# Two more places for weight tiles while the experts run

## The chip, the cores and the metric

One core of one Trainium2 chip runs the program. Its engines work side by side: TensorE (PE in the profile, PEld for its weight loads), VectorE (DVE), ScalarE (ACT), GpSimd (POOL), and SyncE (SP), which here issues the loads to 16 DMA engines. The metric is device time of one launch in microseconds; smaller is better.

## The reference

Two blocks of a network in float32, on 256 tokens of 1024 features and a context of 256 tokens. The first block has two layers: attention with forgetting, then a mixture of experts; retention, then a second mixture of experts. The second block has two layers that mix the tokens (a recurrence over matrices, a spatial gating unit, a convolution), each with a feed-forward; the context goes through a layer and a half of the same.

The experts are what the change is about. A router picks one of 4 groups for a token and 2 of the group's 8 experts; each of the 32 experts is a gated feed-forward of its own:

```python
pg, gi = lax.top_k(p_group, 1)
pv, pi = lax.top_k(jax.nn.softmax(e_in, axis=-1), TOP_K)
gates = pg * pv / jnp.sum(pv, axis=-1, keepdims=True)
# of each expert e, for the tokens xb that chose it:
a, b = jnp.split(xb @ w_gu[e], 2, axis=-1)      # w_gu[e] [1024, 1024]
y = (jax.nn.silu(a) * b) @ w_down[e]            # w_down[e] [512, 1024]
```

The weights of a layer's experts are 32 x 6 MiB, 192 MiB, and they are all read whatever the router picks.

## The kernel before

**Stages.** `run` traces the stages one after the other: `fox` (attention), `moe(0)`, `retention`, `moe(1)`, then the second block for the tokens. `weave` lets side work go along: while `moe(0)` runs, the context's mixing half (`mixer` in mode "f"), and while `moe(1)` runs, the context's feed-forward and the start of its second layer. The text calls this the context's work.

**Experts.** `moe` goes over the experts in 8 groups of 4 (q). For each group it gathers the chosen tokens, 32 places for each expert, features on partitions (`gather`, L895); multiplies them with `w_gu` over 8 row blocks k (L956); takes the gated hidden units (`ha`, L965 and L966), transposes them (L969, L970) and multiplies with `w_down` over 4 row blocks (L976). `combine` (L979) copies the result to SBUF as `ys`, the scaled outputs in the change's words, and adds it to the tokens' rows with a matmul (L986) and an addition (L988). For all but the last group `combine` comes in the middle of the next group's `w_gu` products. `ha` and `ys` each have a tag of their own in the pool `m2`, with two places, 2 KiB per partition each. The last group first asks whether an expert has more than 32 tokens (`overflow`, L1018), with a count that is loaded into registers at L1024; the branch is not taken on these inputs.

**Weight tiles.** Every weight is loaded by SP into a tile of [128, 2048] float32, 1 MiB. The tiles come from `wt` (L126): the pool `wp` has six places, and a load has to wait until a place is free, that is until the last matmul that reads the tile there is done. A pair of loads (`wload2`, L149, the DMA at L153) brings row block k of four experts. Three further places, those of tiles no longer needed, serve once at the start of each `moe` (`self.extra`). The context's loads (`wload`, L132, the DMA at L137) take places from the same pool, and its matmuls are those of L430, L464, L1390 and L1416. The order of loads on SP's queue is fixed when the program is built, and a load that waits holds up all loads behind it.

Of the kernel before, what the change touches and what calls it, by code (L numbers as in the profile page):

```python
# [19 lines left out]
NEG = -1e30  # L20
RS = -8192.0                    # what rsqrt's scaled form carries
NE, CAP, FF = 32, 32, 512
R0, R1, R2, R3, R4 = 1.8, 0.8, 1.0, 0.88, 0.7           # steps of other work per step of the main path
AHEAD = 200                     # instructions that what the others wait for goes ahead of
TAPS = 6                        # convolution taps between other work
PIECE, WS = 512, 6              # elements per partition split at a time; pieces on chip
# [3 lines left out]
# columns of the constant array  # L30
C_ID, C_LE, C_LT, C_GE, C_ONE = 0, 128, 256, 384, 512
C_Z, C_LOW, C_UP = 640, 768, 896          # 0 where col <= row / col >= row, else NEG
C_IOTA, C_GRP, C_I8 = 1024, 1056, 1088
C_SEL, C_OFF = 1096, 1112                 # row 32 j + i, column i; rows of scales: what to add, 1 / RS
C_COS, C_SIN, C_RET = 1116, 1372, 1628         # rotary, decay
NCST = C_RET + 4 * 384

# modulation vectors: which third of the columns of w_mod, and which two of its quarters
# [4 lines left out]
def constants():  # L43
    """Tables that depend on shapes alone."""
# [35 lines left out]
class Tags:  # L80
    """A pool, some of whose tags lie in another one under other names."""
# [10 lines left out]
class Net:  # L92
    def __init__(self, tc, I, out, es):
        self.tc, self.nc, self.I, self.out, self.es = tc, tc.nc, I, out, es
        pool = lambda n, b, **k: es.enter_context(tc.tile_pool(name=n, bufs=b, **k))
        self.cp = pool("cp", 1)
        self.wp = pool("wp", 6)
        self.sm = pool("sm", 2)
        self.dp = pool("dp", 1, space=bass.MemoryType.DRAM)
        self.pg = pool("pg", 4, space=PSUM)  # L100
        self.pm = pool("pm", 2, space=PSUM)
        self.flip, self.extra = 0, []
        self.later, self.pending, self.taken = [], [], False
        self.early, self.hold = -99, None                  # pieces of weights whose low parts GpSimd makes

# [7 lines left out]
    def bank(self):  # L113
        """One bank, from the other pool while g's are taken."""
        return self.m()[:, 0:512] if self.taken else self.g()

    def two(self, mode, apart=False):
        """Two banks."""
# [7 lines left out]
    def wt(self, name):  # L126
        """A weight tile; some lie in the places of tiles that are no longer needed."""
        if self.extra:
            return self.pre.tile([P, 2048], F32, tag=self.extra.pop(0), name=name)
        return self.wp.tile([P, 2048], F32, tag="w", name=name)  # L130

    def wload(self, src):  # L132
        """One tile of weights: rows (k p) of src on the partitions."""
# [6 lines left out]
    def wtile(self):  # L140
        """A weight tile as [P, 2, D]."""
        return self.wt("w").rearrange("p (b d) -> p b d", b=2)

    def gain(self, src, g):
        """src [D] on all partitions."""
# [3 lines left out]
    def wload2(self, src):  # L149
        """The same rows of two experts: src [2, P, 1024]."""  # L150
# [16 lines left out]
    def affine(self, o, i, scale, bias=None, eng=None):  # L167
        """o = i * scale + bias, per partition."""
# [10 lines left out]
    def split(self, pool, tag, src, shape=None, low=None):  # L179
        """src = H + L exactly, both in the tensor engine's one-pass format."""  # L180
# [12 lines left out]
    def wparts(self, w, mode):  # L193
        """Parts of a weight tile [P, k, c]: each a function of (row block, first column, last column)."""
# [15 lines left out]
    def pairs(self, a, b):  # L210
        """Products that make up a.b for operands in parts."""
        return [(a[0], b[0])] if len(a) == 1 else [(a[0], b[0]), (a[1], b[0]), (a[0], b[1])]

    def rstd(self, ss, n, eps=EPS):
        """1/sqrt(ss/n + eps)"""
# [4 lines left out]
    def rsqrt(self, h, scaled=False):  # L220
        """1/sqrt(h): a first guess from the exponent's bits, then Newton's steps. Scaled: RS times it, for one column."""
# [9 lines left out]
        for _ in range(3):  # L231
            if scaled:                  # y = c / sqrt(h) to (y h y - 3 c c) y = -2 c^3 / sqrt(h)
# [13 lines left out]
    def rms(self, x, b, junk, act=False):  # L246
        """rstd of token block b of x [P, 2, D]"""
# [12 lines left out]
    def transposed(self, xn, b, cb):  # L260
        """cb(k, psum [P, n, 128]) for the feature chunks k .. k + n of token block b of xn [P, 2, D]"""
# [7 lines left out]
    def normed(self, pool, x, g, sh, mode, junk, tag="x", first=None, xn=None):  # L269
        """Parts of (rms-normalised x, times g plus sh)^T, each [P, 8, T]; sh and g / RS [P, D].  # L270
        With first = (f, f f, f g), x is replaced by its rms norm with gain f before. Junk: [P, D], or [P, 2, D] with first."""
# [5 lines left out]
        for b in range(2):  # L277
            if b and self.pending:
                self.settle(mark)
            with self.tc.high_priority(offset=(2 - b) * AHEAD):  # L280
# [15 lines left out]
                if first is not None:  # L296
                    # x / sqrt(a); then its own rstd: 1 / sqrt(ss' / (n a) + eps) / sqrt(a)
# [21 lines left out]
    def raw(self, pool, x, g, tag="x", late=False):  # L319
        """Parts of (x times g)^T, each [P, 8, T], g [P, 8]; and the tokens' rstd, [P, 2] and along the free axis, which is  # L320
        left to the products."""
# [40 lines left out]
    def replace(self, after):  # L362
        """The replacing of x that normed has left."""
# [5 lines left out]
    def residual(self, x, o, g, b, wait):  # L369
        """x + o g, once the first tokens are through when waiting"""  # L370
# [15 lines left out]
    def sixteen(self, pool, xin, wsrc, bias, mode, rs=None):  # L386
        """16 columns wsrc [1024, 16], times the tokens' rs, plus bias [P, 16]: [P, 2, 16], in two steps."""
# [4 lines left out]
        # four groups of columns of the array side by side, each with a quarter of the products  # L392
# [24 lines left out]
    def fs(self, xin, wsrc, cb, mode, between=None, middle=None):  # L417
        """Features on partitions: cb(chunk, psum [P, T]) for each 128 columns of wsrc [1024, n]."""
# [18 lines left out]
    def ts(self, xin, wsrc, cb, mode, nk=8, width=512, fresh=False, between=None):  # L437
        """Tokens on partitions: cb(token block, first column, psum [P, width]).
        Fresh: one block of tokens before the other, which may be late."""
# [32 lines left out]
    def logsig(self, z, shape, tag):  # L472
        """log(sigmoid(z)) = min(z, 0) - log1p(exp(-|z|))"""
# [7 lines left out]
        v.scalar_tensor_tensor(c, u, -1.0, e, op0=ALU.add, op1=ALU.subtract)   # (u - 1) - e  # L481
# [29 lines left out]
    def setup2(self):  # L511
        """Small vectors that come later."""
# [16 lines left out]
        # silu(c), silu(c_ctx) as columns 2 n and 2 n + 1 of 32, for each third n of w_mod  # L529
# [36 lines left out]
    def row_vectors(self, l, pool):  # L566
        """Vectors that lie along the free axis, on all partitions."""
# [14 lines left out]
    def fox(self):  # L582
        nc, I = self.nc, self.I
        w_in, w_out = I["fox_w_in"][0], I["fox_w_out"][0]
        with ExitStack() as es:
# [9 lines left out]
            # halves of the heads  # L595
# [17 lines left out]
            # forget logits -> c = cumsum(log sigmoid)  # L613
# [21 lines left out]
            # two more rows for q and k: (c_q, 1) and (1, -c_k)  # L635
# [36 lines left out]
    def fox_heads(self, fp, f2, qa, ka, va, ot, masks):  # L672
        nc, v = self.nc, self.nc.vector
        parts = ((0, 128), (128, 384))          # query blocks with the keys they see
# [54 lines left out]
    def choose(self, mp, L):  # L729
        """L [P, 2, 40]: 4 group logits, 4 of -LOW, 32 expert logits. Membership M [P, 2, 32] of each token's two experts,  # L730
        and what the gates need: sorted logits and indices."""
# [27 lines left out]
    def spread(self, out, gi, w8):  # L759
        """[P, 2, 32] with w8 in the chosen group and 0 elsewhere."""  # L760
# [5 lines left out]
    def gates_of(self, mp, gv, gi, ev, ei):  # L766
        """p_group * p_expert / (sum of the two p_expert), at the experts' places."""
# [27 lines left out]
    def route(self, l):  # L795
        """Loads for the router of layer l."""
# [14 lines left out]
    def route_half(self, l, half, junk):  # L811
        """The router's products for one half of the features; junk [P, 512]."""
# [22 lines left out]
    def logits(self, mp):  # L835
        """The router's logits [P, 2, 40] and the tokens' rstd: products of x itself, scaled by it."""
# [11 lines left out]
    def moe(self, l):  # L848
        nc, I, x, v = self.nc, self.I, self.x, self.nc.vector
        w_gu, w_down = I["expert_w_gu"][l], I["expert_w_down"][l]  # L850
        with ExitStack() as es:
            pool = lambda n, b: es.enter_context(self.tc.tile_pool(name=n + str(l), bufs=b))
            mp, m2 = pool("mp", 1), pool("m2", 2)
            pair = lambda q, k: [self.wload2(w_gu[4 * q + 2 * j:4 * q + 2 * j + 2, k * P:(k + 1) * P, :]) for j in range(2)]
# [6 lines left out]
            # normalised tokens, without the gain  # L861
# [4 lines left out]
            # place of each token among its expert's  # L866
# [18 lines left out]
            def gather(q, n=4):  # L885
                """Tokens of 4 experts, features on partitions; after each step n chunks more."""
# [26 lines left out]
            def placed(q):  # L913
                """Gates at the tokens' places, places on partitions."""
# [13 lines left out]
            for q in range(8):  # L928
# [50 lines left out]
                def combine(y, c0, eng, sgt=sgt):  # L979
                    """Adds y, columns c0 and on, to the places' tokens."""  # L980
                    n = y.shape[1]
                    ys = m2.tile([P, n], F32, tag="ys", name="ys")
# [19 lines left out]
                # the last: one quarter of the columns after the other  # L1002
                ya, yb = y, self.m()
                for c in range(4):
# [10 lines left out]
                    if c % 2:  # L1015
                        yield

    def overflow(self, l, mp, m2, xn, gov, cnti, gain):  # L1018
        """Tokens beyond the CAP places of an expert: that expert densely over all tokens."""
# [44 lines left out]
    def retention(self):  # L1064
        nc, I, x, v = self.nc, self.I, self.x, self.nc.vector
        w_in, w_out = I["ret_w_in"][0], I["ret_w_out"][0]
        with ExitStack() as es:
# [16 lines left out]
            for dst, c0 in ((qr, 0), (kr, 1024)):  # L1084
                hold = []

                def rot(j, ps):
# [3 lines left out]
                    # halves of a head: t1 | t2  # L1091
# [10 lines left out]
            # decayed scores, keys on partitions: [k0: q0 q1 | k1: q1]  # L1102
# [14 lines left out]
            def normal(i):  # L1117
                """The parts of two heads' outputs, features on partitions."""
# [51 lines left out]
    def bn(self, src):  # L1170
        """Mean and variance along the free axis."""
# [6 lines left out]
    def centred(self, src, o):  # L1178
        """o[:, b, :] = src[b] without its mean and over its deviation along the free axis"""
# [12 lines left out]
    def mods(self, l, thirds=(0, 1, 2)):  # L1192
        """silu(c) @ w_mod + b_mod for both conditions i, in blocks of 512 columns: quarter j of third n in row
# [644 lines left out]
```

## Time and profile before

| what | value |
|---|---|
| runs | 2346.77, 2349.72, 2353.5 us; median 2349.72 |
| profiled execution | 2346.0 us from the first to the last instruction (its span); the page gives no other time of it |
| TensorE busy | 2127.2 us, 91% |
| VectorE, ScalarE, GpSimd busy | 1060.9, 695.6, 172.9 us |
| moved by DMA | 686.64 MB, mean 293 GB/s |
| issues of expert weights | 256 of `w_gu` and 112 of `w_down` of 1024 KB, 32 of `w_down` of 512 KB |

Where the experts run is seen from the first and the last matmul of L956: 214.3 to 1611.8 us, in two stages with retention between. A window row gives the length of a stretch, then the busy time and the count of instructions for PE, PEld, DVE, ACT and POOL, the granted TensorE clock as a share, the mean busy share of the 16 DMA engines (packets overlap a little, so it can come out above 1) and the rate. A wait row gives who waited, on which line, for whom, the sum in us, how many times, and the longest.

### The profile page before, as it was taken

What the parts mean: (1) busy time and instruction counts of PE and PEld (TensorE: products, weight loads), DVE (VectorE), ACT (ScalarE), POOL (GpSimd) and SP (SyncE); (2) the same over time, 40 slices, a digit from 0 to 9 for tenths busy, and PEclk for the clock granted to TensorE, in tenths of its full rate; (3) what the DMA queues carried; (4) which work ended last, traced back from release to release, by engine and by line L of the source; (5) the groups of instructions that cost most, each with busy time, mean ns of one, the idle gap of its engine ahead of it and who ended that gap; (6) DMA issues with size and microseconds to landing.
All of it is one profiled execution on the core that took longest, in us unless ns stands there. A gap on an engine that the chain in (4) does not pass through costs nothing. (4 is left out here: it accounts for less than half of the span.)

```text
span 2346.0 us, 32803 instructions
## 1 busy us (share of the span) xinstructions
PE 2127.2 (91%) x12844; PEld 1433.4 (61%) x12845; DVE 1060.9 (45%) x2513; ACT 695.6 (30%) x1420; POOL 172.9 (7%) x194
## 2 busy tenths in 40 slices
PE   8998899889877999989899999987998998998998
PEld 7765445344222776855444444334787997787997
DVE  6556053322101766531121221415778556777555
ACT  4353111211000434520000000012555554554554
POOL 1001000000000111010000000001212002102000
PEclk9999999999988999989999999999999999999999
DMA  8864999999999977579999999999756554555551
GB/s 257 313 245 166 350 399 392 369 399 378 379 409 384 323 281 246 203 268 382 391 398 393 399 390 390 367 356 346 256 162 202 188 190 156 187 181 171 192 185 63
DMA packets 305320, 686.64 MB, mean 293 GB/s; under 512 B 22056, under 2 KB 163784, under 8 KB 298888
## 3 DMA queue, kind: packets, MB, share of 16 engines
q1 hardware_dynamic: 305096, 684.45, 79.9%
q8 instruction: 103, 1.69, 0.3%
q14 instruction: 57, 0.47, 0.1%
q10 hardware_dynamic: 64, 0.03, 0.0%
HBM read 681.78 MB, written 2.62 MB: 292 GB/s over the span
## 5 line engine op out<-in xcount | busy, mean ns | idle before, releaser
L190 DVE TENSOR_TENSOR wl<-w,wh 128x512 fp32r<-128x512 f32 x574 | 396.3, 707 | 252.4 <-ACT wh L185 233.7
L185 ACT CAST wh<-w 128x512 fp32r<-128x512 f32 x600 | 364.3, 621 | 355.5 <-PE psm L430 111.6
L956 PE MATMUL psm<-w,xg 128*32 128x512 f32 x2048 | 319.8, 632 | 61.8 <-DMA w<-in_expert_w_gu_dram 55.0
L430 PE MATMUL psg<-xt,w 128*128 128x256 f32 x1056 | 235.8, 381 | 20.5 <-DMA w<-in_w_gu_dram 11.3
L430 PEld LDWEIGHTS psg<-xt,w 128*128 128x128 f32 x1056 | 198.0, 190 | 71.1 <-issue 38.6
L956 PEld LDWEIGHTS psm<-w,xg 128*32 128x32 f32 x2048 | 66.4, 112 | 270.6 <-issue 150.4
L430 PE MATMUL psg<-xh,wh 128*128 128x256 f32 x608 | 177.2, 291 | 3.9 <-ACT wh L185 2.4
L430 PE MATMUL psm<-xh,wh 128*128 128x256 f32 x640 | 179.9, 281 | 0.6 <-ACT ffh L1450 0.6
L430 PE MATMUL psm<-xh,wl 128*128 128x256 f32 x640 | 179.8, 281 | 0.0
L430 PE MATMUL psm<-xl,wh 128*128 128x256 f32 x640 | 179.7, 281 | 0.0
L430 PE MATMUL psg<-xh,wl 128*128 128x256 f32 x608 | 175.1, 288 | 2.4 <-DVE wl L190 2.4
L430 PE MATMUL psg<-xl,wh 128*128 128x256 f32 x608 | 173.8, 286 | 0.0
L976 PE MATMUL psm<-w,hT 128*32 128x512 f32 (+1 forms) x1152 | 156.7, 564 | 16.0 <-DMA w<-in_expert_w_down_dram 12.5
L430 PEld LDWEIGHTS psg<-xh,wh 128*128 128x128 f32 x608 | 118.1, 194 | 18.6 <-ACT wh L185 9.5
L430 PEld LDWEIGHTS psm<-xh,wh 128*128 128x128 f32 x640 | 120.7, 189 | 1.9 <-ACT ffh L1450 1.1
L430 PEld LDWEIGHTS psm<-xh,wl 128*128 128x128 f32 x640 | 120.6, 188 | 0.7
L430 PEld LDWEIGHTS psg<-xh,wl 128*128 128x128 f32 x608 | 118.0, 194 | 4.9 <-DVE wl L190 4.2
L430 PEld LDWEIGHTS psm<-xl,wh 128*128 128x128 f32 x640 | 120.8, 189 | 0.0
L430 PEld LDWEIGHTS psg<-xl,wh 128*128 128x128 f32 x608 | 117.9, 194 | 0.3 <-issue 0.2
L965 ACT ACTIVATE ha<-psm 128x512 f32<-128x512 f32 x16 | 9.6, 597 | 334.3 <-PE psm L956 334.3
L988 DVE TENSOR_TENSOR x<-x,psg 128x512 f32<-128x512 f32 (+1 forms) x72 | 45.1, 628 | 123.2 <-PE psg L986 123.0
L976 PEld LDWEIGHTS psm<-w,hT 128*32 128x32 f32 x1152 | 38.6, 111 | 93.2 <-issue 52.2
(497 smaller groups left out, 3263.9 us busy)
## 6 DMA issues: line engine op xcount, KB each, us to landing
w<-in_expert_w_gu_dram SPq DMA_DIRECT2D x256, 1024.0 KB
w<-in_expert_w_down_dram SPq DMA_DIRECT2D x112, 1024.0 KB
w<-in_w_gu_dram SPq DMA_DIRECT2D x66, 1024.0 KB
w<-in_w_mod_dram SPq DMA_DIRECT2D x48, 1024.0 KB
w<-in_w_in_dram SPq DMA_DIRECT2D x40, 1024.0 KB
w<-in_w_down_dram SPq DMA_DIRECT2D x33, 1024.0 KB
w<-in_ret_w_in_dram SPq DMA_DIRECT2D x24, 1024.0 KB
w<-in_fox_w_in_dram SPq DMA_DIRECT2D x16, 1024.0 KB
```

The costliest lines, as they stand in the source:

```text
L185: nc.scalar.copy(h, src)
L190: eng.tensor_tensor(l, src, h.bitcast(F32), op=ALU.subtract)
L430: self.nc.tensor.matmul(o, a, x, start=i == 0, stop=i == len(mm) - 1)
L956: nc.tensor.matmul(gu[32 * j:32 * j + 32, half * 512:(half + 1) * 512], xg[:, k, 32 * j:32 * j + 32], ws[j // 2][:, j % 2, half * 512:(hal ...
L965: nc.scalar.activation(ha, gu[:, 0:512], AF.Silu)
L976: nc.tensor.matmul(o[32 * j:32 * j + 32, :], hT[:, k, 32 * j:32 * j + 32], w(j), start=k == 0, stop=k == 3)
L988: v.tensor_tensor(o, o, ps, op=ALU.add)
```

## The change

`wt` takes its place from a list, `self.ring`, in turns. Outside of `moe` the list holds `wp` six times. In `moe` a new pool `more` with two places of a weight tile (16 KiB per partition) is opened after `mp` and `m2`, and the list is six times `wp`, then twice `more`; it is set back at the end of `moe`. `ys` takes the tag of `ha`, so its two places of 2 KiB fall away. The rest of the diff removes comments.

```diff
@@ class Net, __init__
         self.flip, self.extra = 0, []
+        self.ring, self.turn = [self.wp] * 6, 0
@@ wt
         if self.extra:
             return self.pre.tile([P, 2048], F32, tag=self.extra.pop(0), name=name)
-        return self.wp.tile([P, 2048], F32, tag="w", name=name)
+        self.turn = (self.turn + 1) % len(self.ring)
+        return self.ring[self.turn].tile([P, 2048], F32, tag="w", name=name)
@@ moe
             mp, m2 = pool("mp", 1), pool("m2", 2)
+            self.ring = [self.wp] * 6 + [pool("more", 2)] * 2
...
                     n = y.shape[1]
-                    ys = m2.tile([P, n], F32, tag="ys", name="ys")
+                    ys = m2.tile([P, n], F32, tag="ha", name="ys")
...
+            self.ring = [self.wp] * 6
```

## Rows read from the trace of the kernel before

**Rows 1.** The page: DMA share in tenths and rate, in 40 slices.
```profile
DMA  8864999999999977579999999999756554555551
GB/s 257 313 245 166 350 399 392 369 399 378 379 409 384 323 281 246 203 268 382 391 398 393 399 390 390 367 356 346 256 162 202 188 190 156 187 181 171 192 185 63
```

**Rows 2.** Windows of the first experts' stage: full stretches and dips.
```profile
205.00:220.00 15.00, 10.39 (x70) 6.78 (x74) 10.19 (x59) 5.77 (x14) 1.47 (x4) 0.70 0.24 77
235.00:255.00 20.00, 20.00 (x88) 7.86 (x86) 1.81 (x3) 2.02 (x3) 0.76 (x2) 1.00 0.75 269
255.00:425.00 170.00, 153.92 (x954) 86.54 (x954) 62.88 (x199) 31.09 (x73) 3.64 (x8) 0.99 1.02 396
425.00:445.00 20.00, 18.08 (x112) 7.05 (x104) 12.73 (x42) 6.25 (x24) 1.19 (x1) 1.00 0.76 289
575.00:580.00 5.00, 5.00 (x34) 1.59 (x35) 1.86 (x3) 0.00 (x0) 0.00 (x0) 1.00 0.62 203
605.00:610.00 5.00, 5.00 (x33) 1.51 (x35) 1.46 (x3) 0.00 (x0) 0.00 (x0) 1.00 0.45 144
610.00:770.00 160.00, 118.58 (x663) 36.66 (x656) 15.97 (x31) 9.81 (x23) 0.16 (x2) 0.88 1.03 396
```

**Rows 3.** Windows of the second experts' stage.
```profile
1009.00:1018.00 9.00, 9.00 (x63) 3.56 (x62) 4.09 (x22) 0.51 (x2) 1.47 (x4) 0.79 0.17 38
1030.00:1050.00 20.00, 20.00 (x114) 14.37 (x116) 2.06 (x6) 2.90 (x5) 0.76 (x2) 1.00 0.80 281
1075.00:1080.00 5.00, 5.00 (x41) 2.19 (x39) 0.75 (x2) 0.00 (x0) 0.00 (x0) 1.00 0.63 219
1080.00:1482.00 402.00, 372.06 (x1946) 194.63 (x1942) 86.83 (x146) 22.61 (x54) 3.03 (x8) 1.00 1.03 394
1500.00:1545.00 45.00, 41.22 (x178) 17.24 (x178) 19.60 (x37) 6.36 (x15) 4.47 (x4) 0.96 0.80 304
```

**Rows 4.** Waits of SP's queue over the whole run.
```profile
SPq L153 <- PE psm L956: 289.9, 147, 9.4
SPq L153 <- PE psg L430: 223.6, 32, 8.9
...
SPq L1024 <- DVE cnti L912: 19.5, 2, 10.3
```

**Rows 5.** TensorE's waits in 255:425, 445:575, 580:605, 610:770, 1080:1482, 1482:1632, one row each.
```profile
PE psm L956 <- DMA w<-in_expert_w_gu_dram: 5.8, 7, 1.5
...
PE psm L956 <- DMA w<-in_expert_w_gu_dram: 9.5, 9, 2.0
...
PE psm L956 <- DMA w<-in_expert_w_gu_dram: 2.6, 1, 2.6
...
PE psm L956 <- DMA w<-in_expert_w_gu_dram: 25.4, 23, 2.0
...
PE psm L956 <- DMA w<-in_expert_w_gu_dram: 11.8, 15, 1.6
...
PE psg L430 <- DMA w<-in_w_in_dram: 1.2, 1, 1.2
```

**Rows 6.** Timeline, start and length: scaled outputs read, next hidden units written.
```profile
430.20 1.98 PE L986 MATMUL psg<-ys,sgt 128*128 128x512 f32 x4
...
466.55 0.60 ACT L965 ACTIVATE ha<-psm 128x512 f32<-128x512 f32 x1 [28.72 <-PE psm L956]
```

**Rows 7.** SP's queue: the count load (min/median/max ns, first and last start), loads around it.
```profile
L1024 SPq TENSOR_LOAD <-cnti x2: 453/462/472, 215.3 to 1011.0; - x2
...
203.72 0.53 SPq L137 DMA_DIRECT2D w<-in_w_in_dram  x1
...
218.82 5.33 SPq L153 DMA_DIRECT2D w<-in_expert_w_gu_dram  x4
```

**Rows 8.** Loads of line 137 in 200:759 and in 996:1597.
```profile
L137 SPq DMA_DIRECT2D w<-in_w_in_dram x12: 367/368/1102, 203.7 to 532.1; - x12
...
L137 SPq DMA_DIRECT2D w<-in_w_gu_dram x22: 367/368/532, 999.2 to 1455.8; - x22
```

## The prediction

> **What bounds the kernel now.** I read the 40 slices first. A slice is 58.65 us. The DMA row stands at 9 in ten slices from 234 us and again in ten from 1056 us, with rates of 323 to 409 GB/s; all other slices have 313 or less [rows 1]. These two stretches are the experts' stages, with what is prefetched behind them. So if loads bound the kernel anywhere, they do it there. The windows of the first stage [rows 2] then show two kinds of stretch. In 255 to 425 the DMA share is 1.02 at 396 GB/s while TensorE is busy 153.9 of 170 us: loads set the pace. In 235 to 255, 425 to 445, 575 to 580 and 605 to 610 the share is 0.75, 0.76, 0.62 and 0.45 with TensorE busy nearly all the time: the tiles are full, TensorE is on the context's work, and nobody fetches. The second stage has the same pattern at 1009 to 1018, 1030 to 1050, 1075 to 1080 and 1500 to 1545, with 402 us at share 1.03 between [rows 3]. The waits of the DMA queue name the cause: SP stands most often at line 153, the experts' loads, until a matmul that reads an older tile is done, for L956 289.9 us and for L430 223.6 [rows 4]. TensorE's waits are the other half. After each dip it waits for weights again: 5.8 us in 255 to 425, 9.5 in 445 to 575, 2.6 in 580 to 605 and 25.4 in 610 to 770; in the second stage 11.8 in 1080 to 1482 [rows 5]. So the DMA engines idle when the six places are full, and TensorE starves a little later. What the engines fail to fetch in a dip is paid in the next starved stretch, if that is long enough.
>
> **What two more places can bring.** No load, matmul or byte is added or removed. One tile is 1 MiB, 1.0486 MB; at 396 GB/s [rows 2] it takes 2.65 us, two take 5.3. With two more places the queue runs on for up to 5.3 us into each dip. A dip gives back the smaller of 5.3 us and what it lost, once between two starved stretches. I count as lost (1.02 less the share) times the length.
> - Start of stage one, 205 to 255: 15 x 0.78 = 11.7 and 20 x 0.27 = 5.4, in all 17.1; capped at **5.3**. Spent in 255 to 425, where the waits of one line alone are 5.8 [rows 5].
> - 425 to 445: 20 x 0.26 = **5.2**, just under the cap. Spent in 445 to 575 (9.5).
> - 575 to 580: 5 x 0.40 = **2.0**. Spent in 580 to 605 (2.6).
> - 605 to 610: 5 x 0.57 = **2.9**. Spent in 610 to 770 (25.4), and from there the share is 1.03 to the stage's end [rows 2], so all that was won reaches that end.
> - Start of stage two: 9 x 0.85 = 7.7, 20 x 0.22 = 4.4 and 5 x 0.39 = 2.0, in all 14.1 with no starved stretch between; capped at **5.3**. Spent in 1080 to 1482 (11.8 on one line).
> - 1500 to 1545: 45 x 0.22 = 9.9 lost, counted as **0**. After 1482 TensorE waits for loads only 1.2 us, once [rows 5]; other work sets the pace there, and nothing is left to spend the lead on. Its bounds are 0 and the cap, 5.3; I take 0, the end that the 1.2 is nearest to.
>
> Sum: 5.3 + 5.2 + 2.0 + 2.9 + 5.3 = 20.7 us. The profiled execution spans 2346.0 us; the median of the three runs, 2349.7, is 3.7 above that, which I keep as what lies around the span. 2346.0 - 20.7 + 3.7 = **2329 us**.
>
> **What the change costs.** The scaled outputs move into the tag of the gated hidden units, so three tiles per group of four experts share two places of one size. The new neighbour costs nothing as long as each tile is read long before its place comes round again: one block of matmuls on scaled outputs starts at 430.20 and lasts 1.98 us, and the next hidden units are written at 466.55, 34 us later [rows 6]. Were that cover gone, a write would stand behind at most one such block, 2 us, sixteen times: 32 us at most, and it cannot be a gain. I take 0, the end that the 34 us speak for. The two new places lie where the part before the experts kept its last tiles, and a load into them has to wait for the readers of those. In stage one that can cost the first of the two idle stretches, 11.7, but the second, 5.4, is enough for the cap; so 0, with 5.3 as the other end if both were missed. After the stage the loads take turns on the six again. The last eight expert tiles now hold eight places instead of six, so a place among the six comes free no later than today: 0, and one tile's 2.65 us either way.
> The added wait is SP's: a load whose turn falls on the pair waits for that pair, where before any of six places did. Behind it stand all other loads, since the weights are issued on that one queue, and behind those TensorE. This is the price of the last rival.
> The first extra loads must also get past the count load (L1024), at which SP stood 19.5 us in two waits, the longer 10.3 [rows 4], until 215.3 and 1011.0; in stage one four expert loads come right after it, the first at 218.82 [rows 7]. If the extra two stay behind it, the stages' first idle stretches stay, but those of 235 to 255 and of 1030 to 1080 lie after it (5.4 and 4.4 + 2.0 us), and each still fills the cap.
> What is late next in the starved stretches is again the load, at 2.65 us each, since the lead is spent there; past 1482 us it is the context's work.
>
> **A rule that speaks against it.** The share of 1.02 to 1.03 over 160 and 402 us says that the 16 DMA engines themselves are the limit there [rows 2, 3]. The Trainium skill, Perfetto Trace Analysis, section What "DMA-bound" means, says that a kernel bound on DMA engines is helped by large descriptors; places for tiles are not in its list. By that rule alone nothing is won, and it is the second rival below. The trace agrees with it inside the full stretches, and disagrees in the dips, where the share is 0.45 to 0.76.
>
> **The rivals.**
> 1. Only the dips inside stage one pay, and the leads at the two starts are lost: TensorE is busy 20.00 of 20 us there [rows 2, 3], and if the stages are paced by TensorE for longer than the shares say, a load that is early there is early for nobody. Then 5.2 + 2.0 + 2.9 = 10.1 us: 2346.0 - 10.1 + 3.7 = 2339.6. For it: TensorE is busy 372.1 of 402 us in stage two. Against it: it still waits 11.8 us there for one kind of load.
> 2. The change doesn't do what it says: both stages take their bytes over their rate, the lead is never built or is spent on loads that nobody waits for, and the time stays at 2349.7. For it: share 1.02 to 1.03 for most of both stages. Against it: the SP waits [rows 4] and the dips.
> 3. Slower: fixed turns block the queue. The context's loads share the turns: of the two commonest kinds the queue issued 12 in stage one and 22 in stage two [rows 8]; a quarter of these 34, eight or nine, would fall on the pair. If such a tile is held long (the one issued at 203.72 [rows 7] waits for the context's first matmuls), the next turn finds one place of two, and SP stands with free places elsewhere. SP's longest single wait on a context matmul at line 153 is 8.9 us [rows 4]; less the lead of 5.3, 3.6 us each, 8.5 x 3.6 = 31 us lost against 20.7 won: 2349.7 + 10 = 2360. It decides from 20.7 / 8.5 = 2.4 us per such tile. Against it: tiles are read almost in the order of their loads, so what a turn waits for is mostly what is freed next.
>
> **How the numbers follow.** Chances: the forecast 0.60, rival 1 0.20, rival 2 0.11, rival 3 0.09. The forecast's own range is 2324 (the dip at 1500 pays its cap) to 2336 (one start's lead is lost, and 1.5 us of the others). The range reaches from 2321 to 2348, which takes in rival 1 and stops short of no change; it leaves out about 0.05 below and 0.15 above. A measurement of this kernel can tell 0.3%, 7 us, from no change, that is below 2342.7. The forecast and four fifths of rival 1 are faster: 0.76. The rest of rival 1 (its dips half filled) and rival 2 are the same: 0.15. Rival 3 is slower: 0.09.
>
> **What would show it.** In the changed profile the dip after 425 should be at a share near 1.0, those after 575 and 605 gone, and TensorE's waits on the experts' loads shorter by what the dips gave; SP's waits at line 153 should not grow in length. The first stage should end 15 us earlier and the second 21 us. The prediction is wrong if the dips are filled and the stage ends where it did (rival 2), if only the ends of the starts fail (rival 1), or if new dips appear behind a context tile in the pair (rival 3).

## The result and the profile after

The changed kernel takes 2315.39 us (median of 4 runs, 2315.31 to 2318.41). The kernel before, run beside it, takes 2348.24. The ratio is 0.9861 with the 95% interval [0.9848, 0.9874]. The forecast was 2329.0 with a range of 2321 to 2348: the direction was right, the size was not, and the time lies 5.6 us below the range. The profiled execution spans 2316.6 us against 2346.0; its own run took 2318.41.

Lines 430, 956, 976, 1024 and 153 of before are 432, 959, 979, 1028 and 155 here. First the page's DMA rows, for [rows 1]:

```profile
DMA  8875999999999877689999999998756554555551
GB/s 263 312 250 183 358 399 406 379 400 399 409 406 381 316 269 251 233 289 387 399 402 400 402 396 402 370 380 297 245 170 190 195 187 147 203 181 172 183 182 64
```

The fifth to the twelfth slice, all within stage one, had a mean of 384 GB/s and have one of 394; the mean over the run went from 293 to 296. The bytes are the same, 686.64 MB.

Windows of the changed kernel at the places of [rows 2] (same columns), shifted by what the kernel had won by then (the first two stand unshifted):

```profile
205.00:220.00 15.00, 10.82 (x66) 6.99 (x70) 9.73 (x56) 5.23 (x14) 1.47 (x4) 0.66 0.29 98
235.00:255.00 20.00, 20.00 (x87) 8.04 (x86) 1.81 (x3) 2.11 (x4) 0.96 (x3) 1.00 0.81 287
255.00:420.00 165.00, 150.77 (x958) 86.14 (x957) 63.46 (x199) 31.89 (x76) 3.46 (x7) 1.00 1.03 401
419.00:439.00 20.00, 18.42 (x108) 7.51 (x104) 12.60 (x42) 6.13 (x24) 1.18 (x1) 0.91 0.84 320
564.00:569.00 5.00, 5.00 (x31) 1.69 (x33) 2.22 (x4) 0.00 (x0) 0.00 (x0) 1.00 1.03 410
590.00:595.00 5.00, 5.00 (x31) 1.74 (x33) 2.10 (x4) 0.00 (x0) 0.00 (x0) 1.00 1.03 409
594.00:753.00 159.00, 109.54 (x678) 35.06 (x671) 16.15 (x32) 11.02 (x23) 0.16 (x2) 0.98 1.04 398
```

The dips that stood at 575 and 605 are gone (0.62 and 0.45 have become 1.03). The one at 425 is only shallower, 0.84 for 0.76. And the stretch that looked full moved as well: 401 for 396 GB/s, over 165 us in place of 170 for nearly the same work (958 and 954 matmuls).

The second stage, for [rows 3]:

```profile
992.00:1001.00 9.00, 9.00 (x73) 4.26 (x72) 4.41 (x22) 0.73 (x2) 1.47 (x4) 0.92 0.25 77
1013.00:1033.00 20.00, 20.00 (x120) 14.52 (x120) 1.45 (x4) 2.22 (x4) 0.76 (x2) 1.00 0.77 286
1061.00:1454.00 393.00, 370.47 (x1946) 194.80 (x1942) 86.74 (x146) 22.58 (x54) 3.03 (x8) 1.00 1.03 400
1472.00:1517.00 45.00, 41.35 (x183) 18.25 (x182) 19.73 (x38) 6.78 (x15) 4.47 (x4) 0.96 0.90 339
```

The third row holds the same 1946 matmuls as 1080 to 1482 of before. It takes 393 us in place of 402, at 400 GB/s in place of 394, and the share is 1.03 in both.

SP's waits (columns as in [rows 4]) and TensorE's waits on expert weights in 255:419, 439:564, 592:753 and 1061:1454 (as in [rows 5]; in 565:590 there is none):

```profile
...
SPq L155 <- PE psm L959: 214.6, 122, 9.5
SPq L155 <- PE psg L432: 157.7, 32, 10.0
...
SPq L1028 <- DVE cnti L915: 17.9, 2, 9.4
```
```profile
PE psm L959 <- DMA w<-in_expert_w_gu_dram: 5.5, 6, 1.5
...
PE psm L959 <- DMA w<-in_expert_w_gu_dram: 9.4, 8, 2.1
...
PE psm L959 <- DMA w<-in_expert_w_gu_dram: 29.0, 27, 1.5
...
PE psm L959 <- DMA w<-in_expert_w_gu_dram: 6.6, 9, 1.5
```

SP stands 75.3 and 65.9 us less at the experts' line on the two releasers shown. (The longest row of this view, line 139 on VectorE's `wl`, 515.8 us here and 506.6 before, is left out as in [rows 4]: between 200 and 760 and between 1000 and 1600 only 4.6 us of it fall, in one wait.) TensorE's waits shrink where the stage is paced by both (11.8 to 6.6). At the end of stage one they grow, 25.4 to 29.0, while the granted clock there is 0.98 in place of 0.88 and TensorE is busy 109.54 in place of 118.58 us: loads set the pace, and a faster TensorE waits longer.

**Where the time came from.** Ends of work in the two traces: the last combine of stage one 770.4 to 753.8 (16.6 us), the first matmul of stage two's experts 1010.2 to 993.5 (16.7), the last combine of stage two 1631.8 to 1602.6 (29.2), the end 29.4. So stage one gave 16.6 and stage two 12.5. Finer than that is the lead, worked out from the packets: by how much earlier the same number of bytes had landed than in the kernel before, at the times t of before. In stage one it is 6.0 us at t = 300, 8.0 at 425, 9.5 at 500, 10.2 at 575, 13.0 at 605 and 17.0 at 700. For stage two, less what the kernel had when the stage began:

| t of before, us | 1100 | 1240 | 1300 | 1400 | 1482 |
|---|---|---|---|---|---|
| changed kernel (began 16.7 early) | 6.8 | 8.7 | 9.5 | 11.3 | 12.8 |
| pair in stage two alone (1.2 late) | 6.9 | 8.9 | 9.6 | 11.4 | 13.0 |
| pair at its start alone (2.7 early) | 6.2 | 7.9 | 8.0 | 7.1 | 6.7 |
| pair from its third group on (1.5 early) | 5.7 | 5.9 | 6.6 | 8.4 | 10.0 |
| six places, new tag (1.1 early) | 0.3 | -0.5 | -1.1 | -1.5 | -1.6 |

Between its steps the lead stands still to 0.1 us over stretches of up to 60 us. So it isn't a higher rate of the DMA engines. It is a number of short holes that were there before and are not there now, inside the stretch that stood at 1.03: from 1100 to 1482 the lead grows in seven steps. At six of them the kernel before has fewer than 16 packets open (one for each DMA engine), for 0.1 to 1.8 us at a time and some 10 us in all; the changed kernel never has at the same bytes. One step, 0.4 us at 1200, shows no such hole. Two spots of the kernel before, as windows of 4 and 8 us:

```profile
1386.00:1390.00 4.00, 4.00 (x32) 1.82 (x34) 0.75 (x2) 0.00 (x0) 0.00 (x0) 1.00 0.89 336
1426.00:1434.00 8.00, 8.00 (x48) 3.66 (x47) 1.17 (x3) 0.00 (x0) 0.00 (x0) 1.00 0.86 326
```

And the same work in the changed kernel:

```profile
1360.00:1364.00 4.00, 4.00 (x35) 1.77 (x37) 0.75 (x2) 0.00 (x0) 0.00 (x0) 1.00 1.02 410
...
1398.00:1406.00 8.00, 8.00 (x49) 3.63 (x48) 1.03 (x3) 0.00 (x0) 0.00 (x0) 1.00 1.02 408
```

What makes such a hole is seen in SP's queue. Its timeline in the kernel before (start, length, what is issued):

```profile
1374.69 4.00 SPq L153 DMA_DIRECT2D w<-in_expert_w_down_dram  x3
1379.14 0.37 SPq L137 DMA_DIRECT2D w<-in_w_down_dram  x1
1387.58 3.94 SPq L153 DMA_DIRECT2D w<-in_expert_w_gu_dram  x4
1391.61 0.45 SPq L137 DMA_DIRECT2D w<-in_w_gu_dram  x1
1398.21 5.54 SPq L153 DMA_DIRECT2D w<-in_expert_w_gu_dram  x4
```

Loads go out in bunches of three to five. Between 1379.5 and 1387.6 none goes out, for 8.1 us. At 2.65 us a load that is three loads' worth. By the packets the list ran dry at 1387.9, 8.4 us after the last issue, and was full again at 1389.8, 2.2 us after the next one: with six places it held little more than three loads, and some 10 us were to be covered. The changed kernel at that spot, in the windows 1349:1361 and 1361:1364 of the view:

```profile
1349.04 0.42 SPq L139 DMA_DIRECT2D w<-in_w_down_dram  x1
1352.22 1.19 SPq L155 DMA_DIRECT2D w<-in_expert_w_gu_dram  x2
...
1361.47 2.22 SPq L155 DMA_DIRECT2D w<-in_expert_w_gu_dram  x2
1363.79 0.42 SPq L139 DMA_DIRECT2D w<-in_w_gu_dram  x1
```

The gap is there too, and as long: 8.1 us, from 1353.4 to 1361.5. But two more loads go out before it, 5.3 us of transfer, and the packets never run out. (Seen over a longer window, the view merges these four loads into one row, in which the gap can't be seen.) Over the whole stretch long gaps are also rarer: 16 of 7 us or more between 1080 and 1482, one between 1061 and 1454 of the changed kernel.

### The profile page after: what moved, and what is told of

Its sections match the earlier page's. It is cut to its first block, busy times and chain, and to the rows that moved or that the text cites. A ratio compares the mean times of both kernels' runs of the same rounds, so it can differ in the third digit from the quotient of the medians.

```text
span 2316.6 us, 32809 instructions
## 1 busy us (share of the span) xinstructions
PE 2103.0 (91%) x12844; PEld 1431.6 (62%) x12845; DVE 1061.8 (46%) x2513; ACT 695.5 (30%) x1420; POOL 172.9 (7%) x194
## 2 busy tenths in 40 slices
DMA packets 305320, 686.64 MB, mean 296 GB/s; under 512 B 22056, under 2 KB 163784, under 8 KB 298888
## 5 line engine op out<-in xcount | busy, mean ns | idle before, releaser
L959 PE MATMUL psm<-w,xg 128*32 128x512 f32 x2048 | 300.4, 604 | 56.9 <-DMA w<-in_expert_w_gu_dram 50.5
L959 PEld LDWEIGHTS psm<-w,xg 128*32 128x32 f32 x2048 | 64.9, 110 | 249.8 <-issue 146.7
```

Of the source, the lines that this page charges most:

```text
L959: nc.tensor.matmul(gu[32 * j:32 * j + 32, half * 512:(half + 1) * 512], xg[:, k, 32 * j:32 * j + 32], ws[j // 2][:, j % 2, half * 512:(hal ...
```

## The experiments

**Theory 1**: the deeper list gives the lead at the stages' starts and wide dips, and also fills short holes inside the stretches that looked full. **Theory 2**: only the lead counts; what stage two gained beyond 5.3 us comes from the state in which the stages before hand over. All times are medians; the kernel before stood at 2348.55 (first four kernels), 2349.36 (next four) and 2348.78 (last two).

**The tag alone.**

```diff
-            self.ring = [self.wp] * 6 + [pool("more", 2)] * 2
```


> Only the move of the scaled outputs into the hidden units' tag; six places for weights as before. Both theories: no change, 2348 us within 4. If the shared tag itself is worth something, it shows here as more than 7 us.

Measured: 2348.78 us, ratio 1.0 [0.9985, 1.0014]. The scaled outputs in the hidden units' tag cost and give nothing that can be measured, as taken from [rows 6]. All of the gain is the pair's. In the changed kernel, too, the next hidden units come long after the scaled outputs are read, 31 us after the last of the two blocks ends:

```profile
424.09 1.98 PE L989 MATMUL psg<-ys,sgt 128*128 128x512 f32 x4
...
457.18 0.60 ACT L968 ACTIVATE ha<-psm 128x512 f32<-128x512 f32 x1 [25.46 <-PE psm L959]
```

**The pair in stage one alone.**

```diff
+            self.ring = [self.wp] * 6 + ([] if l else [pool("more", 2)] * 2)
```


> Two more places in the first experts' stage only. Both theories: that stage ends 16.6 us earlier as in the changed kernel, and the rest of the run is as before: 2348.2 - 16.6 = 2331.6 us.

Measured: 2331.08, ratio 0.9927 [0.991, 0.9943], 17.5 us. Stage one ends at 754.0, as in the changed kernel (753.8), and stage two gives nothing. Its groups three to six run as with six places:

```profile
1148.00:1461.00 313.00, 289.60 (x1515) 152.16 (x1513) 67.73 (x114) 17.45 (x42) 2.28 (x6) 1.00 1.03 395
```

**The pair in stage two alone.**

```diff
+            self.ring = [self.wp] * 6 + ([pool("more", 2)] * 2 if l else [])
```


> Two more places in the second experts' stage only. Theory 1 (short dips inside the full stretches are filled too, besides the lead at the stage's start): the whole 12.5 us that the second stage gained in the changed kernel, 2348.2 - 12.5 = 2335.7 us. Theory 2 (only a lead of two tiles, 5.3 us, is won here, and the other 7 us come from the state in which the first stage and retention hand over): 2343 us.

Measured: 2332.15, ratio 0.9931 [0.9915, 0.9948], 16.4 us. Theory 2 falls: stage one ended as before (771.6), so nothing was handed over, and stage two gave 15.9 us by its ends (1.2 late to 14.6 early, rounded). Theory 1's number, 2335.7, was too high as well, by 3.5 us. Groups three to six:

```profile
1158.00:1467.00 309.00, 289.75 (x1518) 152.26 (x1520) 67.95 (x115) 17.45 (x42) 2.27 (x6) 1.00 1.03 401
```

17.5 and 16.4 us add up to 33.9; both together give 32.9. The stages are independent to about 1 us.

**One more place instead of two.**

```diff
+            self.ring = [self.wp] * 6 + [pool("more", 1)]
```


> One more place instead of two, in both stages. Theory 2 (lead alone, capped at one tile of 2.65 us for each dip): 2.65 + 2.65 + 2.0 + 2.65 + 2.65 = 12.6 us, 2335.6 us, and the rate between 1087 and 1477 us stays at 394 GB/s. Theory 1: a short dip needs less than one tile, so one place already fills most of them: the rate of the full stretches is near 400 GB/s, and some 7 us more are won, 2328.6 us.

Measured: 2326.17, ratio 0.9909 [0.9893, 0.9926], 22.4 us. Theory 1 was nearer. The first place gives twice what the second gives (22.4, then 10.8). The full stretch needs only the first:

```profile
1149.00:1456.00 307.00, 288.47 (x1516) 151.64 (x1511) 67.42 (x114) 17.44 (x42) 2.27 (x6) 1.00 1.03 400
```

**The pair at the start of stage two alone.**

```diff
+            self.ring = [self.wp] * 6 + ([pool("more", 2)] * 2 if l else [])
...
             for q in range(8):
                 e0 = 4 * q
+                if q == 2:
+                    self.ring = [self.wp] * 6
```


> The pair is given in stage two alone and only until the third group of experts begins; from there six places again. In the run with the pair in all of stage two the rank before the third group came 7.8 us early against the run with six, and the other 8 us came later. Theory 1 (a deeper list gives a lead once AND keeps the stretches that looked full from running dry for some tenths of a microsecond at a time): only the lead is kept, 2348.6 - 7 = 2341 us (2339 to 2344), and the rate from the third to the seventh group falls back to 394 GB/s with 2 % of the time under 16 open packets. Theory 2 (all comes from the lead, and what showed later is knock-on of it): 2333 us (2331 to 2335).

Measured: 2340.48, ratio 0.9968 [0.9953, 0.9982], 8.9 us: theory 1's number. In the table of leads it wins 7.9 us until 1240 and then loses a little, as the kernel with six does. The stretch and one hole:

```profile
1155.00:1468.00 313.00, 289.64 (x1517) 152.12 (x1517) 67.71 (x114) 17.47 (x42) 2.27 (x6) 1.00 1.03 393
...
1376.00:1380.00 4.00, 4.00 (x32) 1.97 (x35) 0.75 (x2) 0.00 (x0) 0.00 (x0) 1.00 0.88 320
```

**The pair from the third group of stage two on.**

```diff
+            more = pool("more", 2) if l else None
...
+                if q == 2 and l:
+                    self.ring = [self.wp] * 6 + [more] * 2
```


> The complement: stage two with six places until the third group begins, eight from there to its end; stage one with six. Theory 1: the lead at the stage's start is missing, but the stretch of groups three to six runs at 400 instead of 394 GB/s (about 4 us) and the last two groups lose less at their dips (about 4 us): 2348.6 - 8 = 2341 us (2338 to 2344), with no time under 16 open packets there. Theory 2 (only the lead at the start counts, a stretch at share 1.02 has nothing to give): 2348 us (2346 to 2349.5).

Measured: 2333.47, ratio 0.9932 [0.9915, 0.9949], 15.9 us. Neither theory's number: by its time it gives nearly all that the pair gives in the whole stage; by the ends of its trace stage two gave 12.0 us (1.6 early to 13.6 early), against 15.9 with the pair in the whole stage. The edit didn't do what it was meant to. The order in which loads are issued isn't the order in which they are written down: the two first loads into the pair, weights of the third group, wait for no weight tile, and the program issues them as the seventh and ninth expert load of the stage, at 974.5 and 979.9. So the lead at the start is there (5.7 us at 1100), bought with weights that are needed some 185 us later (the third group's first matmul starts at 1162.7). Then the pair is taken until the third group, the table stands still from 1100 to 1240 (5.7 to 5.9), and from there it climbs by 4.1 us to 1482, as in the changed kernel (4.1). Together with the run before this shows the two parts apart: the lead without the holes, and the holes when the pair turns again.

**The context's loads kept out of the pair.**

```diff
-        w = self.wt("w")
+        w = self.wt("w") if len(self.ring) == 6 else self.wp.tile([P, 2048], F32, tag="w", name="w")
```


> Eight places, but the loads of the context's layer never take their turn in the pair; they go round the six alone, so no expert's load stands behind a context tile held in the pair, and the six are taken out of step. If the fixed turns of the changed kernel cost something (a context tile held long in the pair blocks the load queue), this is faster than the changed kernel: 2306 to 2311 us. If they cost nothing, as the waits of the load queue suggest: the changed kernel's 2315 within 3 us. It is slower (2318 to 2325) if the context's loads then crowd the six and hold the queue there instead.

Measured: 2320.74, ratio 0.9878 [0.9861, 0.9894]. Slower than the changed kernel by 5.3 us, though SP's total at the experts' line on L959 is shorter:

```profile
SPq L155 <- PE psm L959: 196.8, 107, 8.8
SPq L155 <- PE psg L432: 155.5, 31, 9.6
```

Sorting the loads this way saves nothing on the whole. At t = 300 this kernel's lead stood 3.1 us below the changed kernel's, and it never came level: 1.5 us were missing at 500 and 1.4 at the start of stage two, 3.3 at 1100. What in the queue's order costs these was not tried. In the dip at 425 alone it won more, 3.1 us of lead against 1.5, at a share of 0.92 in 420 to 440: there, it seems, the context's tiles take up room in the pair. It had come into the dip with less lead, so this isn't shown.

**Five places, first edit.** A tile of the pool is allocated at every fifth load and never used.

```diff
+        if len(self.ring) == 5 and self.turn == 0:
+            self.wp.tile([P, 2048], F32, tag="w", name="none")
```


> Five places instead of six in both stages (every sixth allocation is a tile that nothing uses). Theory 1 (the list runs dry in short stretches as well as at the dips, and each place fewer makes more such stretches): the steps so far are 11 us from eight to seven and 22 us from seven to six, so the next is larger still, 30 to 50 us: 2380 to 2400 us, and the rate of groups three to six falls from 394 GB/s to 375 to 388. Theory 2 (a place is worth only its lead of 2.65 us a stage at a few fixed spots): 2356 to 2362 us, and that rate stays at 394.

Measured: 2349.47, ratio 1.0 [0.9989, 1.0011]. An unused tile takes no place: the experts' loads go round six addresses in this program, as in the one with the tag alone. The run says nothing on five places. It repeats the kernel with six.

**Five places.**

```diff
-        self.wp = pool("wp", 6)
+        self.wp, self.w6 = pool("wp", 5), pool("w6", 1)
...
-            self.ring = [self.wp] * 6 + [pool("more", 2)] * 2
+            self.ring = [self.wp] * 5
...
-            self.ring = [self.wp] * 6
+            self.ring = [self.wp] * 5 + [self.w6]
```


> Five places while the experts run, this time in earnest: the pool of six is parted into five and one, and the experts' loads go round the five alone; elsewhere all six are used, the sixth in a fixed turn. Theory 1 (the loads run dry at many short spots of the expert stages, and each place fewer opens more of them): the steps so far are 11 us from eight to seven and 22 from seven to six, so 30 to 50 us more from six to five: 2380 to 2400 us; the stretch of stage two that looked full (groups three to six, 394 GB/s with six places, 400 with eight) falls below 388. Theory 2 (a place is worth a lead of 2.65 us at a few wide dips only): 2356 to 2362 us, and that stretch stays at 394. A fixed turn of the sixth place outside the expert stages may cost or give some us there, which the ends of the stages tell apart.

Measured: 2424.36 (2411.69 to 2433.26), ratio 1.0302 [1.0271, 1.0332], 75.6 us slower. Theory 1's direction, about twice its size; theory 2 falls again. The profiled run is the slowest of the four. By the ends of its trace against before, stage one is 30.6 us longer and stage two 47.3; some 5 us lie in retention between, where the sixth place has a fixed turn. Second to sixth group of stage two, the waits of TensorE in them, and SP's queue:

```profile
1133.00:1554.00 421.00, 373.20 (x1899) 195.96 (x1902) 81.21 (x138) 22.00 (x53) 3.02 (x8) 0.97 0.96 364
```
```profile
PE psg L432 <- DMA w<-in_w_gu_dram: 21.6, 11, 3.2
PE psm L959 <- DMA w<-in_expert_w_gu_dram: 14.6, 14, 2.8
```
```profile
1457.89 0.37 SPq L139 DMA_DIRECT2D w<-in_w_down_dram  x1
1459.74 2.60 SPq L155 DMA_DIRECT2D w<-in_expert_w_gu_dram  x4
1470.08 0.37 SPq L139 DMA_DIRECT2D w<-in_w_gu_dram  x1
1471.93 4.77 SPq L155 DMA_DIRECT2D w<-in_expert_w_gu_dram  x4
1485.37 0.37 SPq L139 DMA_DIRECT2D w<-in_w_gu_dram  x1
```

The gaps without an issue are as long as before, 7.7 us (1462.3 to 1470.1) and 8.7 (1476.7 to 1485.4), but the list is one load shorter: under 16 packets are open for 18% of the time from 1207 to 1535, against 2% with six places, and only now does the share of a long window show it (0.96). Places against time: five 2424.4, six 2348.8, seven 2326.2, eight 2315.4; steps of 75.6, 22.6 and 10.8 us.

**Eight places, the pair's turns spread.**

```diff
-            self.ring = [self.wp] * 6 + [pool("more", 2)] * 2
+            more = pool("more", 2)
+            self.ring = ([self.wp] * 3 + [more]) * 2
```


> The same eight places, the pair's turns spread: three of the six, one of the pair, three, one, instead of six and then two. If the number of places alone decides: the changed kernel's 2315 within 3 us. If the place of the fixed turns matters (which load meets a tile that a context layer still holds): up to 6 us either way, 2309 to 2321, and the difference stands at the spots where the load queue waits, in stage one above all, where the run without context loads in the pair lost 3 us in its first dip.

Measured: 2315.71 (2314.07 to 2318.84), ratio 0.9855 [0.9838, 0.9871]: the changed kernel's time. With all loads in the ring, the number of places decides and not where the pair's turns stand, as far as these two orders tell. No version tried beats the changed kernel.

## Why the prediction was right and wrong

**Mechanism: right.** The list of loads ran dry because places were taken; two more places let it run on. The new tag is free (2348.78 against 2348.55). The two idle stretches in which the pair might have come too late were long enough.

**Stage one: right in sum, 15.4 forecast, 16.6 by the ends, 17.0 by bytes, and in part by luck.** Term by term, as the lead grew: start 5.3 forecast, 6.0 measured; inside 300 to 425 nothing forecast, 2.0; 425 to 445 5.2, 1.5; 500 to 575 nothing, 0.7; 575 to 580 2.0, 2.8; 605 to 610 2.9, 4.0. The dip at 425 was the one bad term: it lay below the cap and was taken as refilled whole, but the changed kernel still stands at 0.84 in the same work; why the two places did no more there is open. The 3.7 us that it missed were made up by 2.7 us of short holes that the sum didn't have and 2.6 us more on the other three terms.

**Stage two: the step that failed.** "Start of stage two: capped at 5.3" held roughly: 6.8 at 1100. What failed is the stretch of 402 us behind it, which the sum took as having nothing to give because its share was 1.03 [rows 3]. It held 6.0 us of short holes (12.8 less 6.8). Two places fill all of them, one place nearly all, and taking the pair away there brings them back. The share couldn't show them: packets overlap (16.4 were open on the mean, on 16 engines), so a mean of 1.03 over 402 us covers holes of 0.1 to 1.8 us, and 394 GB/s looked like the limit until 400 was seen beside it. The same holes, 2.0 us of them, were in 255 to 425 at 1.02. The dip at 1500, counted 0 between bounds of 0 and 5.3, gave 0.9 in this trace (28.3 us at the seventh group's first matmul, 29.2 at the last combine), though its share went from 0.80 to 0.90: near the 0. It isn't settled: by the same two marks four other kernels with the pair there won 1.6 to 4.0 us, and kernels with six places there lost 0.9 to won 1.6.

**The sum's last term.** The span came to 2316.6 where 2346.0 - 20.7 = 2325.3 was forecast: 8.7 us, of which 1.2 in stage one, 7.2 in stage two, and the rest elsewhere. The other 4.9 us of the miss are the 3.7 that were kept around the span, and 1.2 by which the new median lies below the profiled span. The 3.7 weren't around it: each run of the changed kernel takes 1.8 us more than its span, and the profiled runs differ from their medians, 2346.0 + 1.8 lying 0.4 below the median of before and 2318.41 lying 3.0 above that of after. In the medians the change is worth 32.9 us, in the profiled pair 29.4.

**The rivals.** Rival 1 falls with the pair in stage two alone (16.4 us). Rival 2, no change, rested on the full stretches. The Trainium skill, Perfetto Trace Analysis, section What "DMA-bound" means, names large descriptors as what matters for a kernel bound on its DMA engines. Here the bytes and the loads' sizes stayed as they were and the time fell by 1.4%, so a share of 1.03 did not yet show that state. Rival 3, the queue blocked by fixed turns, didn't come: the longest wait on a context matmul at the experts' line went from 8.9 to 10.0 us, but the total on that line fell from 223.6 to 157.7 (on another context line, L1416 and now L1420, it rose from 68.9 to 79.8), and neither sorting nor spreading the turns gave anything.

**The signs named.** Dips at 575 and 605 gone: yes. Dip after 425 near 1.0: no, 0.84. Stage one 15 us earlier: 16.6. Stage two 21: 29.2. TensorE's waits shorter by what the dips gave: in part in stage two (5.2 us on one line, of 12.5 won), not in stage one, where its clock rose. SP's waits at the experts' line no longer than before: not quite, the longest went from 9.4 to 9.5 and from 8.9 to 10.0 us.

## What to carry to other kernels

A high DMA share over a long window doesn't say that the loads are at their limit: look at windows of a few us inside it, and in the issuing queue compare the longest gap between two bunches of loads (here 8 us, and 2 more until the next load's packets ran) with what the list holds when the gap opens (little more than three loads of 2.65 us each). Ask for single issues there: a merged row hides a gap. Near that point the price of a place is steep and one-sided: 75.6 us for the sixth (some 5 of them outside the experts' stages), 22.6 for the seventh, 10.8 for the eighth. An edit that gives a buffer "from step n on" changes what is issued long before step n, if nothing holds those loads back.

## What was not expected of the hardware

With eight places the 16 DMA engines moved 400 GB/s over the 308 to 309 us of groups three to six in three kernels (the changed one 400, the pair in stage two alone 401, its turns spread 400), with never fewer than 16 packets open on the core. With six places it was 393 to 395, with under 16 packets open for 2 to 3% of the time. The rate while the list was full was the same in both, as the constant lead between the steps shows.
